# FoX attention scores as two fp32r products over split queries and keys, in a one-layer hybrid decoder

## The chip, the cores and the metric
One core of a Trainium2 chip. The metric is device time in microseconds of one execution, as the median of several runs. Engines are called PE (matrix products), ACT (ScalarE), DVE (VectorE), POOL (GpSimd) and SP (which issues most loads). The core's DMA queues move weights in.

## What is computed
One decoder layer for 512 tokens and a width of 1024, in float32. The input is normed and modulated (adaLN) and goes through one projection into three groups of heads: RWKV-7 (4 heads of 64), FoX (6 heads of 64, forgetting attention) and NSA (6 heads of 64 in two groups; compressed, selected and window branches). Their outputs are concatenated and go through an output projection; a gated feed-forward net with a width-3 convolution follows. The part that this change is about, cut:

```python
def fox_mix(p, b_f):
    q, k, v, f_logit = split_cols(p, FOX_COLS)
    log_f = jax.nn.log_sigmoid((f_logit + b_f))
    cum = jnp.cumsum(log_f, axis=1).transpose(0, 2, 1)
    ...
        logits = (jnp.einsum('bhqd,bhkd->bhqk', qb, k) * scale + cb[..., None] - cum[:, :, None, :])
        probs = masked_softmax(logits, kpos[None, :] <= qpos[:, None])
        return jnp.einsum('bhqk,bhkd->bhqd', probs, v)
...
    x = x + g_m * rmsnorm(y, norm_g[l, 1])     # g_m: "gate 0", a row of silu(c) @ ada_w
```

## The kernel before, in words
Weights are split as they come in: hi is the float32 weight in the reduced format fp32r (ACT, `split`, L182), lo is what remains (DVE or POOL by a letter table, BGE, OPE). A projection is three fp32r products per 128 rows (`mm3`: hi hi, lo hi, hi lo), so 24 products of 512 columns for one 128-wide tile of queries or keys (`fm_gen`).

Three stages follow one another. To 55 us the first projections run. To 208 us the RWKV recurrence runs: preparation, an inversion by doubling (`doubling`, `transition`), then eight chunks for two head pairs (`chunks`), in which PE and DVE take turns on 64 x 64 products. `both` advances this chain and after each step takes BG[n] steps of a background generator (the other projections, compression of NSA keys into `hid` and `kcm`/`vcm`, and `token_major`, whose products are 332 columns wide); LG says how far back in PE's list those steps may be tied. The layer's second modulation (`mods_f`, from `in_ada_c`) also runs here, by a letter table (MFE) on DVE, or on POOL and ACT.

To 395 us the attention runs. Pairs of heads come in the order of AO: NSA 0, then n1, f0, f1, then NSA 2 and FoX 2 with the first part of the output projection. A head is `softmax_t`: scores in four tiles (128, 256, 384 and 512 keys, in three banks `qkps`), a minimum with bias added on DVE (L961), exponentials on ACT (L963), then `transposed_p`: scaling of each tile (SCE, L979), transposes on PE (L985, `ptps`), copies of them to `pt` on ACT or DVE (EVE, L412 and L414), and `pv`. After each softmax `fill` takes FN[n] steps of the query and key projections (`gemms`; later `out_parts`) and GN[n] steps of gate 0 (`gate_pe`).

NSA queries and keys are split in fp32r already (`nsa_gen`, `k_stack`): two products over 128 rows give a tile. FoX queries and keys stay float32 over 64 rows:

```python
            def qk(i, ps, q=q):
                mm(ps, fq[q, i * P:(i + 1) * P], fk[q, :ps.shape[1]], True, False)
                mm(ps[:, i * P:], idr, cmr, False, True)
```

A scheduler that knows priorities puts the instructions of each engine in order; the tables and the order of the code are its input.

Of the kernel before, what the change touches and what calls it, by code (L numbers as in the profile page):

```python
# [11 lines left out]
F32 = mybir.dt.float32  # L12
# [8 lines left out]
BGE = 'DPPDDPDPPDPDDPPPDPPD'  # L21
OPE = 'PPDDPP'
MFE = 'DPPPDDPDPPDDPDPP'
WOE = 'DDP'

SCE = 'DDDD'
EVE = 'ADDA'
# [9 lines left out]
BG = [0, 10, 0, 1, 2, 3, 2, 0, 0, 1, 2, 0, 0, 0, 0, 4, 0, 14, 0, 0, 0, 3, 0, 0, 10, 4, 2, 0, 0, 1, 9, 0, 0, 1, 6, 0, 0, 0, 0, 1, 0, 0, 4, 0, 3, 17, 0, 2, 7, 0, 0, 16, 1, 1, 0, 4, 8, 0, 0, 7, 3, 10, 6, 8, 4]  # L37
LG = [1, 2, 1, -1, 0, -1, -1, -1, -1, -1, -1, 2, -1, 2, -1, -1, 1, -1, -1, -1, -1, -1, 2, 1, -1, -1, 1, -1, -1, -1, -1, -1, -1, 2, -1, -1, 1, 2, 2, 2, -1, 2, 2, 2, 2, -1, -1, -1, -1, -1, -1, -1, -1, -1, -1, -1, -1, 1, -1, 0, 0, 0, 0, 0, 0]
PRI = 400

FN = [11, 4, 12, 6, 6, 1, 13, 13, 14, 0, 10, 12, 15, 9, 17, 8, 26, 14]
GN = [4, 16, 4, 0, 10, 0, 9, 5, 18, 3, 6, 0, 5, 8, 0, 8, 13, 7]
AO = ['n1', 'f0', 'f1']
# [4 lines left out]
P = 128  # L48
S = 512
# [41 lines left out]
def trunk(ctx: ExitStack, tc: tile.TileContext, I, out):  # L91
# [38 lines left out]
    def hh(h):  # L130
        return slice(64 * h, 64 * h + 64)
# [108 lines left out]
    def gate_pe(which, dst, pool):  # L240


        for h in range(2):
            def load(k2):
                return wload(I["ada_g"][which, 2 * k2:2 * k2 + 2, :, 0, 512 * h:512 * h + 512].rearrange("k p c -> p k c"),
                             2, 512)
            raw = [load(0), load(1)]
            yield
            raw.append(load(2))
# [6 lines left out]
            rows = pool.tile([P, 512], F32, name="grow", tag="gacc")  # L256
            nc.scalar.copy(rows, ps)
            yield
            ps = bank("mm")
            mm(ps, ones, rows, True, True)  # L260
            gate_rows(which, h, ps, dst, pool, "gb")
            yield
# [743 lines left out]
    def fox_gen(n, j):  # L1006
# [5 lines left out]
    qz = [at(f"qz{n}", (P, 2, S), 1, F32R) for n in range(2)]  # L1012
    for t in qz:
        for h in range(2):
            nc.gpsimd.memset(t[hh(1 - h), h, :].bitcast(F32), 0.0)
# [21 lines left out]
    def fox(j):  # L1037
# [16 lines left out]
        maps = [softmax_t(maps[0])[0], (fill(), softmax_t(maps[1])[0])[1]]  # L1054
        fill()
# [5 lines left out]
    def nsa(j):  # L1061
# [46 lines left out]
        for br, (kx, vc) in enumerate(((ks, TM_VS), (kw, TM_VW))):  # L1108
            maps = []
            for g in range(2):  # L1110
# [3 lines left out]
                def qk(i, ps):  # L1114
# [3 lines left out]
                    mm(ps, qz[j % 2][:, g, ts], kx[1][:, :w], False, True)  # L1118
# [3 lines left out]
                maps.append((softmax_t((qk, bias, gate[:, :, 3 * h + 1 + br]))[0], vc + g * HD))  # L1122
                fill()
# [419 lines left out]
```

## Time and profile before

| | |
|---|---|
| median of 3 runs (lowest, highest) | 799.06 us (798.9, 800.05) |
| profiled execution: its own time | 799.51 us |
| its span in the trace | 797.7 us |
| mean granted PE clock | 0.981 |
| busy: PE, DVE, ACT, POOL | 94%, 58%, 46%, 16% of the span |

Busy shares are averages over stages. A PE instruction's end is modelled, and products overlap, so the time that one takes from PE is read from the start of the next. A wait is put down to the instruction that came last.

### The profile page before, as it was taken

What the parts mean: (1) busy time and instruction counts of PE and PEld (TensorE: products, weight loads), DVE (VectorE), ACT (ScalarE), POOL (GpSimd) and SP (SyncE); (2) the same over time, 40 slices, a digit from 0 to 9 for tenths busy, and PEclk for the clock granted to TensorE, in tenths of its full rate; (3) what the DMA queues carried; (4) which work ended last, traced back from release to release, by engine and by line L of the source; (5) the groups of instructions that cost most, each with busy time, mean ns of one, the idle gap of its engine ahead of it and who ended that gap; (6) DMA issues with size and microseconds to landing.
All of it is one profiled execution on the core that took longest, in us unless ns stands there. A gap on an engine that the chain in (4) does not pass through costs nothing.

```text
span 797.7 us, 11245 instructions
## 1 busy us (share of the span) xinstructions
PE 750.4 (94%) x4326; PEld 589.6 (74%) x4326; DVE 464.5 (58%) x889; ACT 365.7 (46%) x657; POOL 131.4 (16%) x147
## 2 busy tenths in 40 slices
PE   1999897899898999999999999999999999999996
PEld 0875786789574776566588988888888888888885
DVE  4947896433482663687277676676666575223224
ACT  4658253234573562576255654445444434123121
POOL 3031017143403521002152011111110000000001
PEclk9998998999999998999999999999999999999999
DMA  9961339535216621003144243333233333323302
GB/s 345 396 217 55 92 93 197 196 132 205 76 58 209 200 80 53 27 1 106 55 170 130 82 132 107 132 122 105 98 125 132 106 111 114 98 86 106 101 32 106
DMA packets 38902, 99.49 MB, mean 125 GB/s; under 512 B 13652, under 2 KB 13652, under 8 KB 38848
## 3 DMA queue, kind: packets, MB, share of 16 engines
q1 hardware_dynamic: 33520, 86.88, 32.3%
q0 software_dynamic: 5328, 11.89, 5.1%
q8 instruction: 34, 0.56, 0.3%
q14 instruction: 20, 0.16, 0.1%
HBM read 94.76 MB, written 5.94 MB: 126 GB/s over the span
## 4 chain that ended last, share of the span: by engine, by line
PE 86%; DMA 5%; ACT 3%; DVE 3%; issue 1%; POOL 1%; SPq 0%; DVEq 0%; POOLq 0%; ACTq 0%
PE mmps L104 44%; PE smps L104 13%; PE gmps L104 9%; PE accps L104 7%; PE qkps L104 5%; PE wops L104 5%; PE ptps L985 2%; DMA raw<-in_ada_c 2%; DMA raw<-in_ada_g 1%; DMA x_sb<-in_x 1%; DMA raw<-in_w_fm 1%; ACT whi L182 1%; PE cpps L104 0%; POOL rstd L284 0%; DVE hid L523 0%
## 5 line engine op out<-in xcount | busy, mean ns | idle before, releaser
L182 DVE TENSOR_TENSOR wlo<-raw,whi 128x1024 fp32r<-128x1024 f32 (+2 forms) x86 | 111.6, 1301 | 130.8 <-ACT whi L182 130.5
L182 ACT CAST whi<-raw 128x1024 fp32r<-128x1024 f32 (+3 forms) x102 | 104.3, 1025 | 121.6 <-PE mmps L104 63.5
L104 PE MATMUL mmps<-h2hi,whi 128*128 128x512 f32 (+1 forms) x352 | 133.0, 378 | 0.6 <-ACT h2hi L182 0.6
L104 PE MATMUL mmps<-h2lo,whi 128*128 128x512 f32 (+1 forms) x352 | 132.1, 375 | 0.2 <-DVE h2lo L182 0.2
L104 PE MATMUL mmps<-h2hi,wlo 128*128 128x512 f32 (+1 forms) x352 | 131.9, 375 | 0.0
L104 PEld LDWEIGHTS mmps<-h2hi,whi 128*128 128x128 f32 x352 | 66.2, 188 | 13.2 <-ACT h2hi L182 0.9
L104 PEld LDWEIGHTS mmps<-h2lo,whi 128*128 128x128 f32 x352 | 66.2, 188 | 13.1 <-DVE h2lo L182 0.6
L104 PEld LDWEIGHTS mmps<-h2hi,wlo 128*128 128x128 f32 x352 | 66.2, 188 | 11.9
L182 POOL TENSOR_TENSOR wlo<-raw,whi 128x1024 fp32r<-128x1024 f32 (+2 forms) x16 | 36.9, 2309 | 129.7 <-ACT whi L182 120.7
L272 POOL TENSOR_TENSOR ggf<-ggf,raw 128x1024 f32<-128x1024 f32 x7 | 16.8, 2404 | 145.4 <-ACT raw L271 145.4
L104 PE MATMUL mmps<-whi,hhi 128*128 128x332 f32 (+1 forms) x96 | 34.0, 354 | 0.0
L412 ACT COPY pt<-ptps 128x256 f32<-128x256 f32 (+1 forms) x36 | 16.7, 479 | 37.6 <-PE ptps L985 28.9
L104 PE MATMUL mmps<-whi,hlo 128*128 128x332 f32 (+1 forms) x96 | 33.5, 349 | 0.0
L1396 ACT ACTIVATE gt<-gt 128x512 f32<-128x512 f32 x22 | 13.9, 632 | 42.4 <-DVE gt L1381 42.4
L104 PE MATMUL mmps<-wlo,hhi 128*128 128x332 f32 (+1 forms) x96 | 33.3, 347 | 0.0
L104 PE MATMUL accps<-pt,tm 128*64 128x512 f32 (+3 forms) x144 | 31.0, 442 | 1.4 <-ACT pt L412 1.4
L104 PE MATMUL gmps<-hhi,whi 128*128 128x512 f32 x72 | 30.2, 419 | 1.0 <-ACT nq L1020 1.0
L292 POOL TENSOR_TENSOR rstd<-rstd,mhalf 128x1 f32<-128x1 f32 x8 | 7.0, 873 | 136.6 <-DVE rstd L291 136.6
L104 PE MATMUL gmps<-hlo,whi 128*128 128x512 f32 x72 | 29.0, 402 | 0.0
L104 PE MATMUL gmps<-hhi,wlo 128*128 128x512 f32 x72 | 28.8, 400 | 0.0
L414 DVE COPY pt<-ptps 128x384 f32<-128x384 f32 (+1 forms) x36 | 14.3, 418 | 23.9 <-PE ptps L985 15.4
L225 POOL TENSOR_TENSOR raw<-raw,crow 128x1024 f32<-128x1024 f32 x9 | 21.2, 2366 | 24.9 <-DMA raw<-in_ada_c 23.2
(515 smaller groups left out, 1723.2 us busy)
## 6 DMA issues: line engine op xcount, KB each, us to landing
raw<-in_up SPq DMA_DIRECT2D x44, 512.0 KB, 3.5
raw<-in_ada_c SPq DMA_DIRECT2D x32, 512.0 KB, 9.2
raw<-in_down SPq DMA_DIRECT2D x22, 512.0 KB, 3.4
raw<-in_ada_g SPq DMA_DIRECT2D x16, 512.0 KB, 3.5
raw<-in_w_fm SPq DMA_DIRECT2D x14, 512.0 KB, 5.2
raw<-in_w_out SPq DMA_DIRECT2D x11, 512.0 KB, 3.8
raw<-in_w_k SPq DMA_DIRECT2D x8, 384.0 KB, 9.3
x_sb<-in_x SPq DMA_DIRECT2D x4, 512.0 KB, 9.3
```

The lines of the kernel that those rows point to most:

```text
L104: pe.append(nc.tensor.matmul(o, lhsT, rhs, start=start, stop=stop))
L182: return nc.scalar.copy(hi, src), eng.tensor_tensor(lo, src, hi.bitcast(F32), op=ALU.subtract)
L225: nc.gpsimd.tensor_tensor(raw[n], raw[n], crow, op=ALU.mult)
L272: nc.gpsimd.tensor_tensor(dst, dst, raw, op=ALU.add)
L292: nc.gpsimd.tensor_tensor(r, r, mhalf, op=ALU.pow)
L412: nc.scalar.copy(dst, src)
L414: nc.vector.tensor_copy(dst, src)
L985: nc.tensor.transpose(ps[:, o:o + P], s_[:, kt * P:(kt + 1) * P], ident)
L1396: nc.scalar.activation(gt, gt, AF.Silu)
```

## The change
FoX queries and keys are written as two-half tiles. A query tile holds, for each head of the pair, fp32r queries on the head's 64 rows and their remainder on the other 64. The key tile fk holds the fp32r keys on both halves, fkl the keys' remainder on the head's rows and zeros elsewhere. So fq x fk gives hi hi + lo hi and fq x fkl gives hi lo. fq, fk, qs and qz now have one buffer each, and their writers wait until the previous pair's scores are issued. Gate 0 is made in four quarters of 256 columns, from two loads each that are both asked for a step ahead, rather than in halves from four loads. The order is n0, f0, n1, f1, n2, f2, and all tables are new.

```diff
-BGE = 'DPPDDPDPPDPDDPPPDPPD'
-OPE = 'PPDDPP'
-MFE = 'DPPPDDPDPPDDPDPP'
+BGE = 'PPDDDPPDPDPDDPDPPPDP'
+OPE = 'DDDPDD'
+MFE = 'DDPPPDDDPDDDDPPP'
-SCE = 'DDDD'
-EVE = 'ADDA'
+SCE = 'AAAD'
+EVE = 'AADA'
...
-FN = [11, 4, 12, 6, 6, 1, 13, 13, 14, 0, 10, 12, 15, 9, 17, 8, 26, 14]
-GN = [4, 16, 4, 0, 10, 0, 9, 5, 18, 3, 6, 0, 5, 8, 0, 8, 13, 7]
-AO = ['n1', 'f0', 'f1']
+FN = [11, 0, 11, 9, 17, 1, 24, 4, 22, 0, 15, 22, 26, 6, 16, 23, 34, 19]
+GN = [1, 0, 2, 1, 1, 1, 0, 1, 0, 1, 1, 2, 0, 0, 1, 0, 0, 0]
+AO = ['f0', 'n1', 'f1']
...
-        for h in range(2):
-            def load(k2):
...
-                if k == 6:
-                    raw.append(load(3))
-                mm(ps[g, :], sc32[:, k:k + 1].to_broadcast([P, 32]), raw[k // 2][:, k % 2, :], k < 4, k >= 4)
+        for c in range(4):
+            cs_ = slice(256 * c, 256 * c + 256)
+            raw = [wload(I["ada_g"][which, 4 * n:4 * n + 4, :, 0, cs_].rearrange("k p c -> p k c"), 4, 256) for n in range(2)]
...
+                mm(ps[g, 0:256], sc32[:, k:k + 1].to_broadcast([P, 32]), raw[k // 4][:, k % 4, :], k < 4, k >= 4)
...
+    fkl = at("fkl", (P, 2, S), 1, F32R)
+    qz = at("qz", (P, 2, S), 1, F32R)
...
     def fox_gen(n, j):
         ps = yield from fm_gen(I["w_fm"][(FM_FQ if n == "fq" else FM_FK) + j])
-        t = at(n, (P, S), 2)
-        nc.scalar.activation(t, ps, AF.Copy, scale=-0.125 if n == "fq" else 1.0)
+        while j and ("f", j - 1) not in fqk:
+            yield
+        t = at(n, (P, 2, S), 1, F32R)
+        for h in range(2):
+            src = ps[hh(h), :]
+            if n == "fq":
+                nc.scalar.mul(t[hh(h), h, :], src, -0.125)
+                nc.vector.scalar_tensor_tensor(t[hh(1 - h), h, :], src, -0.125, t[hh(h), h, :].bitcast(F32),
+                                               op0=ALU.mult, op1=ALU.subtract)
+            else:
+                nc.scalar.copy(t[hh(h), h, :], src)
+                nc.scalar.copy(t[hh(1 - h), h, :], src)
+                nc.vector.tensor_tensor(fkl[hh(h), h, :], src, t[hh(h), h, :].bitcast(F32), op=ALU.subtract)
         fqk[n, j] = t
...
-            def qk(i, ps, q=q):
-                mm(ps, fq[q, i * P:(i + 1) * P], fk[q, :ps.shape[1]], True, False)
+            def qk(i, ps, hp=hp):
+                q, w = fq[:, hp, i * P:(i + 1) * P], ps.shape[1]
+                mm(ps, q, fk[:, hp, :w], True, False)
+                mm(ps, q, fkl[:, hp, :w], False, False)
                 mm(ps[:, i * P:], idr, cmr, False, True)
```

First place, PE, the scores of one FoX head (second head of pair 0) and what stands around them. `cmr,idr` is the mask, `ptps` are transposes. Before:

```order
L985 MATMUL ptps<-ident,s__2725 128x128 x3
L104 MATMUL qkps<-fk,fq 128x128
L104 MATMUL qkps<-cmr,idr 128x128
L104 MATMUL qkps<-fk,fq 128x256
L104 MATMUL qkps<-cmr,idr 128x128
L104 MATMUL qkps<-fk,fq 128x384
L104 MATMUL qkps<-cmr,idr 128x128
L104 MATMUL qkps<-fk,fq 128x512
L104 MATMUL qkps<-cmr,idr 128x128
L985 MATMUL ptps<-ident,s__2725 128x128 x4
```

Of the change:

```order
L104 MATMUL qkps<-fk,fq 128x128
L104 MATMUL qkps<-fkl,fq 128x128
L104 MATMUL qkps<-cmr,idr 128x128
L104 MATMUL qkps<-fk,fq 128x256
L104 MATMUL qkps<-fkl,fq 128x256
L104 MATMUL qkps<-cmr,idr 128x128
L104 MATMUL qkps<-fk,fq 128x384
L104 MATMUL qkps<-fkl,fq 128x384
L104 MATMUL qkps<-cmr,idr 128x128
L104 MATMUL qkps<-fk,fq 128x512
L104 MATMUL qkps<-fkl,fq 128x512
L104 MATMUL qkps<-cmr,idr 128x128
```

Each tile has a second product, with fkl, between the first and the mask.

Second place, PE, NSA pair 0, from the last tiles of its second head's scores on (`gmps` is a projection). Before:

```order
L104 MATMUL qkps<-kh,qs 128x384
L104 MATMUL qkps<-lk,qz_2042 128x384
L104 MATMUL qkps<-kh,qs 128x512
L104 MATMUL qkps<-lk,qz_2042 128x512
L104 MATMUL gmps<-hhi,whi 128x512
L104 MATMUL gmps<-hlo,whi 128x512
L104 MATMUL gmps<-hhi,wlo 128x512
```

Of the change:

```order
L104 MATMUL qkps<-kh,qs 128x384
L104 MATMUL qkps<-lk,qz 128x384
L104 MATMUL qkps<-kh,qs 128x512
L104 MATMUL qkps<-lk,qz 128x512
L104 MATMUL qkps<-kh,qs 128x128
L104 MATMUL qkps<-lk,qz 128x128
L104 MATMUL qkps<-kh,qs 128x256
L104 MATMUL qkps<-lk,qz 128x256
```

Before, 20 projection products follow and then the third head; now the third head and most of the fourth follow at once, and 22 projection products after them.

Third place, PE, in the last chunks of the RWKV loop (`s` is the state, `mmps` with 332 columns the filler). Before:

```order
L104 MATMUL smps<-r_1007,mt 64x64
L104 MATMUL smps<-s_1895,tmpa 64x64
L104 MATMUL smps<-r_1007,mt 64x64
L104 MATMUL smps<-s_1895,tmpa 64x64
L104 MATMUL mmps<-whi,hlo 128x332
L104 MATMUL mmps<-whi,hhi 128x332
L104 MATMUL mmps<-wlo,hhi 128x332
L104 MATMUL mmps<-whi,hlo 128x332
```

Of the change:

```order
L104 MATMUL smps<-r_1007,mt 64x64
L104 MATMUL smps<-s_1893,tmpa 64x64
L104 MATMUL smps<-r_1007,mt 64x64
L104 MATMUL smps<-s_1893,tmpa 64x64
L104 MATMUL smps<-tok 64x64
L104 MATMUL smps<-am,tmpb 64x64
L104 MATMUL smps<-tmpb,tok 64x64
L104 MATMUL smps<-am,tok 64x64
```

Ten filler products stand here before and none now. Of the 192 products of 332 columns, 13 stood ahead of the first doubling products, 46 between there and the chunk loop and 133 in the loop; now it is 40, 56 and 96.

## Rows read from the trace of the kernel before

**Rows 1.** The page: busy time, share of the span and instructions of each engine; the chain of work that ended last, by engine.

```profile
PE 750.4 (94%) x4326; PEld 589.6 (74%) x4326; DVE 464.5 (58%) x889; ACT 365.7 (46%) x657; POOL 131.4 (16%) x147
PE 86%; DMA 5%; ACT 3%; DVE 3%; issue 1%; POOL 1%; SPq 0%; DVEq 0%; POOLq 0%; ACTq 0%
```

**Rows 2.** Busy time of each engine in three stages (us from the span's start; instructions in brackets), then the clock, DMA share and GB/s.

```profile
55.00:208.00 153.00, 137.12 (x1466) 112.90 (x1466) 92.08 (x184) 70.70 (x126) 49.32 (x41) 0.94 0.50 146
208.00:395.00 187.00, 180.74 (x868) 119.31 (x868) 110.33 (x351) 100.78 (x248) 32.13 (x47) 0.97 0.25 82
395.00:797.70 402.70, 394.98 (x1838) 328.81 (x1836) 225.70 (x285) 164.01 (x231) 38.71 (x32) 1.00 0.33 110
```

**Rows 3.** What PE waited for, 118 to 208 us: us in total, times, longest.

```profile
PE cpps L104 <- DVE hid L527: 5.2, 1, 5.2
PE smps L104 <- ACT tmpb L791: 2.6, 1, 2.6
```

**Rows 4.** PE's instructions in order of time (start us, us; float32 products stand as two records): the last tile of a FoX head at full clock and what follows, then a head from its first tile to what follows it.

```profile
298.84 1.12 PE L104 MATMUL qkps<-fk,fq 64*128 64x512 f32 x2
299.89 0.33 PE L104 MATMUL qkps<-cmr,idr 128*128 128x128 f32 x1
300.15 1.05 PE L104 MATMUL mmps<-nq,kcm 64*32 64x512 f32 x4
...
303.90 0.48 PE L104 MATMUL qkps<-fk,fq 64*128 64x128 f32 x2
304.32 0.33 PE L104 MATMUL qkps<-cmr,idr 128*128 128x128 f32 x1
...
306.55 1.83 PE L104 MATMUL qkps<-fk,fq 64*128 64x512 f32 x2
308.31 0.47 PE L104 MATMUL qkps<-cmr,idr 128*128 128x128 f32 x1
```

**Rows 5.** The same view: the scores of an NSA head between two projection products.

```profile
228.33 0.39 PE L104 MATMUL gmps<-hlo,whi 128*128 128x512 f32 x1
228.56 0.22 PE L104 MATMUL qkps<-kh,qs 128*128 128x128 f32 x1
228.62 0.28 PE L104 MATMUL qkps<-lk,qz 128*128 128x128 f32 x1
228.73 0.33 PE L104 MATMUL qkps<-kh,qs 128*128 128x256 f32 x1
...
229.83 0.40 PE L104 MATMUL gmps<-hhi,wlo 128*128 128x512 f32 x1
```

**Rows 6.** The same view: gate 0's products (x12 is six float32 products, x4 is two), with PE's idle time ahead of them and what ended it.

```profile
233.99 1.91 PE L104 MATMUL mmps<-raw,sc 128*32 128x512 f32 x12
238.52 1.05 PE L104 MATMUL mmps<-raw,sc 128*32 128x512 f32 x4 [0.23 <-DMA raw<-in_ada_g]
...
250.70 1.05 PE L104 MATMUL mmps<-raw,sc 128*32 128x512 f32 x4 [2.73 <-DMA raw<-in_ada_g]
```

**Rows 7.** What PE waited for, 208 to 395 us: us in total, times, longest.

```profile
PE mmps L104 <- DMA raw<-in_ada_g: 3.0, 2, 2.7
PE accps L104 <- ACT pt L412: 1.4, 3, 0.7
```

**Rows 8.** The instructions on one head's probabilities: ns shortest/median/longest of its four tiles, first and last start, forms.

```profile
L961 DVE CUSTOM_DVE_ANT_0 s__2139<-qkps,bias x4: 292/486/693, 220.8 to 222.2; 128x128 f32<-128x128 f32 x1, 128x256 f32<-128x256 f32 x1, 128x384 f32<-128x384 f32 x1, 128x512 f32<-128x512 f32 x1
L963 ACT ACTIVATE s__2139<-s__2139,mn x4: 402/550/715, 221.2 to 223.4; 128x128 f32<-128x128 f32 x1, 128x256 f32<-128x256 f32 x1, 128x384 f32<-128x384 f32 x1, 128x512 f32<-128x512 f32 x1
L979 DVE TENSOR_SCALAR s__2139<-s__2139,sm x4: 287/380/479, 225.8 to 226.6; 128x128 f32<-128x128 f32 x1, 128x256 f32<-128x256 f32 x1, 128x384 f32<-128x384 f32 x1, 128x512 f32<-128x512 f32 x1
```

**Rows 9.** ACT, 208 to 396 us, groups by form: count, busy us, mean ns of one, idle time before.

```profile
L412 ACT COPY pt<-ptps 128x512 f32<-128x512 f32 x18 | 10.6, 586 | 28.5 <-PE ptps L985 28.4
L412 ACT COPY pt<-ptps 128x256 f32<-128x256 f32 x18 | 6.7, 371 | 9.1 <-PE accps L104 8.5 <-PE ptps L985 0.5
...
L1009 ACT ACTIVATE fq<-gmps 128x512 f32<-128x512 f32 x3 | 1.8, 595 | 4.9 <-PE qkps L104 4.7 <-PE gmps L104 0.2
...
L1083 ACT COPY sp<-mmps 64x512 f32<-64x512 f32 x3 | 1.7, 575 | 3.1 <-PE mmps L104 3.1
```

**Rows 10.** The view of rows 2, in four slices: after the granted clock stand the DMA's share and GB/s.

```profile
136.00:140.00 4.00, 4.00 (x53) 3.58 (x51) 0.39 (x2) 2.46 (x6) 0.00 (x0) 0.55 0.94 266
308.00:312.00 4.00, 4.00 (x14) 3.30 (x14) 1.94 (x9) 2.79 (x8) 0.27 (x1) 0.50 0.00 0
312.00:316.00 4.00, 4.00 (x16) 3.17 (x15) 1.45 (x5) 0.95 (x4) 0.27 (x1) 0.79 0.24 70
372.00:376.00 4.00, 4.00 (x16) 3.25 (x16) 0.82 (x3) 0.63 (x2) 0.00 (x0) 0.61 0.52 188
```

**Rows 11.** PE in order of time, around its two long waits in the RWKV stage.

```profile
135.71 0.43 PE L104 MATMUL cpps<-more,hid 128*32 128x64 f32 x4 [5.19 <-DVE hid L527]
...
151.67 0.31 PE L104 MATMUL mmps<-wlo,hhi 128*128 128x332 f32 x1
151.82 0.31 PE L104 MATMUL mmps<-whi,hlo 128*128 128x332 f32 x1
154.75 1.15 PE L104 MATMUL smps<-mt,tmpb 64*64 64x64 f32 x32 [2.61 <-ACT tmpb L791]
```

**Rows 12.** DVE in order of time: a copy in the chunk loop.

```profile
198.44 0.22 DVE L844 COPY tmpb<-smps 128x64 f32<-128x64 f32 x1 [1.18 <-PE smps L104]
```

More of the change, by code (lines that the diff above doesn't have):

```diff
@@ L240, in gate_pe @@
     def gate_pe(which, dst, pool):
-        for h in range(2):
-            def load(k2):
-                return wload(I["ada_g"][which, 2 * k2:2 * k2 + 2, :, 0, 512 * h:512 * h + 512].rearrange("k p c -> p k c"),
-                             2, 512)
-            raw = [load(0), load(1)]
+        for c in range(4):
+            cs_ = slice(256 * c, 256 * c + 256)
+            raw = [wload(I["ada_g"][which, 4 * n:4 * n + 4, :, 0, cs_].rearrange("k p c -> p k c"), 4, 256) for n in range(2)]
             yield
-            raw.append(load(2))
             ps = bank("mm")
             for k in range(KT):
-                if k == 6:
-                    raw.append(load(3))
                 g = slice(32 * (k % 4), 32 * (k % 4) + 32)
-                mm(ps[g, :], sc32[:, k:k + 1].to_broadcast([P, 32]), raw[k // 2][:, k % 2, :], k < 4, k >= 4)
-            rows = pool.tile([P, 512], F32, name="grow", tag="gacc")
-            nc.scalar.copy(rows, ps)
+                mm(ps[g, 0:256], sc32[:, k:k + 1].to_broadcast([P, 32]), raw[k // 4][:, k % 4, :], k < 4, k >= 4)
+            if c % 2 == 0:
+                rows = pool.tile([P, 512], F32, name="grow", tag="gacc")
+            nc.scalar.copy(rows[:, 256 * (c % 2):256 * (c % 2) + 256], ps[:, 0:256])
             yield
[L259 to L262, printed above, removed]
+            if c % 2:
+                ps = bank("mm")
+                mm(ps, ones, rows, True, True)
+                gate_rows(which, c // 2, ps, dst, pool, "gb")
+                yield
     def gate_pool(which, dst, pool, tag):
@@ L1004, in trunk @@
     fqk = {}
+    fkl = at("fkl", (P, 2, S), 1, F32R)
+    qz = at("qz", (P, 2, S), 1, F32R)
+    for t in (fkl, qz):
+        for h in range(2):
+            nc.gpsimd.memset(t[hh(1 - h), h, :].bitcast(F32), 0.0)
     def fox_gen(n, j):
         ps = yield from fm_gen(I["w_fm"][(FM_FQ if n == "fq" else FM_FK) + j])
-        t = at(n, (P, S), 2)
-        nc.scalar.activation(t, ps, AF.Copy, scale=-0.125 if n == "fq" else 1.0)
+        while j and ("f", j - 1) not in fqk:
+            yield
+        t = at(n, (P, 2, S), 1, F32R)
+        for h in range(2):
+            src = ps[hh(h), :]
[7 more added lines that the diff above has]
+                nc.vector.tensor_tensor(fkl[hh(h), h, :], src, t[hh(h), h, :].bitcast(F32), op=ALU.subtract)
         fqk[n, j] = t
[L1012 to L1015, printed above, removed]
     def nsa_gen(j):
         ps = yield from fm_gen(I["w_fm"][FM_NQ + j])
+        while j and ("n", j - 1) not in fqk:
+            yield
         nq = at("nq", (P, S), 1)
         nc.scalar.mul(nq, ps, -0.125)
-        qs = at("qs", (P, 2, S), 2, F32R)
+        qs = at("qs", (P, 2, S), 1, F32R)
         for h in range(2):
             nc.scalar.copy(qs[hh(h), h, :], nq[hh(h), :])
-            nc.scalar.copy(qz[j % 2][hh(h), h, :], nq[hh(h), :])
+            nc.scalar.copy(qz[hh(h), h, :], nq[hh(h), :])
             nc.vector.tensor_tensor(qs[hh(1 - h), h, :], nq[hh(h), :], qs[hh(h), h, :].bitcast(F32), op=ALU.subtract)
@@ L1054, in fox @@
         maps = [softmax_t(maps[0])[0], (fill(), softmax_t(maps[1])[0])[1]]
+        fqk["f", j] = True
         fill()
@@ L1117, in qk @@
                     mm(ps, qs[:, g, ts], kx[0][:, g, :w], True, False)
[L1118 removed]
+                    mm(ps, qz[:, g, ts], kx[1][:, :w], False, True)
                 def bias(i):
@@ L1122, in nsa @@
                 maps.append((softmax_t((qk, bias, gate[:, :, 3 * h + 1 + br]))[0], vc + g * HD))
+                if br and g:
+                    fqk["n", j] = True
                 fill()
```

5 lines of the change are left out of this document (2 added, 3 removed).

## The prediction
> **What bounds the kernel now.** I read the page first, then the stages, then the waits, then single heads. TensorE (PE) is busy for 94% of the span and the chain of work that ended last runs over PE for 86% of it [rows 1], so whatever leaves PE's list shortens the kernel unless a wait takes its place. The diff touches two of three stages [rows 2]: 55 to 208 us (the RWKV recurrence, with projections as filler) and 208 to 395 us (FoX and NSA attention). What follows 395 us has the same rows in the same order on PE and is taken as unchanged, as are the first 55 us. In the attention stage PE is busy 180.7 of 187 us, ScalarE (ACT) 100.8 and VectorE (DVE) 110.3: PE is the limit with little idle time. In the RWKV stage PE is idle 15.9 of 153 us, and two waits make up half of that [rows 3].
>
> **The FoX scores.** A head's scores are four tiles of 128 to 512 keys. Now each is one float32 product over 64 rows, then the mask product. In a head at a low clock for only its last tile, PE needs 2.65 us from the first tile to the fourth; at full clock the fourth takes 1.05 us and its mask 0.26 us [rows 4]. So a head costs 3.96 us. The two products that replace it already stand in NSA: same format (fp32r), same widths, 128 rows, two per tile. A whole NSA head runs in 1.27 us [rows 5]. I take that for the new FoX head, and add four fp32r masks of 128 columns at the spacing of NSA's 128-wide products (0.06 to 0.11 us, together 0.35 us). The new head costs 1.6 us and saves 2.35 us; six heads save **14.0 us**. The bounds are 7.6 us (first rival) and 16 us (some old heads ran at a lower clock).
>
> The page FP8 and Floating Point Precision of the Trainium skill (TensorE Precision Notes) says that true FP32 takes four passes through the array. By passes alone an old head would be twice an NSA head's time, 2.54 us, and the gain over six heads 7.6 us, an estimate by that page. The rows give 3.96 us, masks included, so the trace holds more than the passes.
>
> **Gate 0.** A group of six products takes 1.9 us and one of two takes 1.05 us [rows 6]: about 1 us for up to four products, which go to four strips of 32 output rows. Both halves make 5.9 us. Now there are four quarters, each two groups of four at half the width: 4 x 2 x 0.5 = 4.2 us at most. That saves **1.7 us** (bounds 0 and 2.5). PE also waited 3.0 us for these loads [rows 6, 7]. Each quarter's loads are now asked for a step ahead, but quarters 0 and 1 stand only one FoX head (1.6 us) and some transposes apart and there are three raw buffers, so I count half of the wait as saved, **1.5 us** (0 to 3).
>
> **What is added beside PE.** The tables move three of four scalings of each head (SCE) and the 128-wide copy of P transposed (EVE) from DVE to ACT, and the queries and keys are now split there. ACT copies of 512 and 256 columns take 0.586 and 0.371 us [rows 9], a slope that puts 384, 256 and 128 columns at 0.48, 0.37 and 0.26 us, 1.11 us for a head's three scalings. The nearest ACT instruction with a factor per row is the exponential, whose lower three widths (0.40 us at 128 to 0.72 us at 512, [rows 8]) would make 1.5 us. Eighteen heads: 20 to 27 us. The 128-wide copies add 18 x 0.26 = 4.8 us. Splitting adds 18 copies of 64 x 512 at 0.575 us and drops six at 0.595 us [rows 9]: 6.8 us. ACT gains 32 to 39 us, I take 35: 136 us in a stage of some 175 us. DVE loses about 15 us net, the same scalings being 0.29 to 0.48 us there [rows 8]; the three w_out splits that go from GpSimd (POOL) to DVE stay within that.
>
> With 86 idle us on ACT before and some 39 after, not all of this stays hidden. I price the new waits of PE at **+7 us**, in three places. First, the scores of three NSA heads now follow one another with no projection between (second order excerpt): a head's reductions on DVE take 0.29 to 0.69 us each, 1.95 us in all [rows 8], against 1.27 us on PE, and there are three score banks; 2 us (0 to 3). Second, the first FoX head needs fkl, which DVE makes after ACT's copy of the same half; both stand behind what their queues already hold, and only a score tile, transposes and a gate group lie between the key projection and its use: 1.5 us. Third, the transposes of a head now wait for scalings that stand in ACT's queue behind other heads' exponentials: a tenth of the 35 us, 3.5 us. Bounds: 2 us (the projections cover nearly all) and 35 us (none is covered; a rival).
>
> What I cost at nothing: single buffers for fq, fk, qs and qz, since their writers wait only for a previous head pair's scores, and the order shows whole projections (24 products, 5.5 us) elsewhere in between; with that cover gone it would be a projection's evacuation, 2.3 us, five times. FoX 0 now stands before NSA 1, so its bias must come through DRAM sooner: POOL's stores and loads of it move ahead of NSA 1's table loads. Between the transposes of the gate logits and the next FoX products stand a projection (24 x 0.23 us, [rows 5]) and PV products, over 5.5 us, which cover a scan and two short transfers; without cover 5 us.
>
> **The clock.** Four slices of 4 us ran at 0.50 to 0.79 of the clock although PE was busy all through [rows 10]; beside the full clock they cost 0.45 x 4 + 0.50 x 4 + 0.21 x 4 + 0.39 x 4 = 6.2 us. Three follow FoX scores. If half-filled float32 products set this off, they are gone; but PE will also wait more. I take **2 us** gained (0 to 6).
>
> **The RWKV stage.** Before the first doubling products there were 13 projection products of 332 columns, now 40. These 27, at 0.15 us each [rows 11], fill 4.1 of the 5.2 us in which PE waited for hid. Between there and the chunk loop 56 stand in place of 46, in front of the second wait (2.6 us, for ACT's tmpb [rows 3, 11]): 24 of them in one group where 8 were; 2.4 us. The chunk loop keeps 96 of 133, and its last three chunks have none (third order excerpt). A bare step there waits for a DVE copy of 0.22 us [rows 12] and its two semaphores, some 0.3 us, and six bare steps cost 2 us. Net **4.5 us** gained; bounds are 8 us (all of both waits) and 3 us lost. SP's loads are asked for in nearly the same order. POOL's split of the second w_tm part now stands ahead of the loads of the inverted tiles; 2.3 us of POOL work, hidden by those 27 products, and 2 us if it isn't.
>
> **Sum.** 14.0 + 1.7 + 1.5 - 7 + 2 + 4.5 = 16.7 us gained. The profiled execution took 799.5 us (span 797.7 and 1.8 around it), which gives 782.8; the median of the runs is 0.45 lower, so **782.5 us**. A measurement of this kernel can tell about 0.2% (1.6 us) from no change.
>
> **Rivals.**
> (a) Only the passes go: what float32 costs over four passes is due to switching formats around the scores and remains. Against it: NSA heads among the same neighbours run 1.27 us. For it: the switch to float32 transposes is still there. FoX gains 7.6, not 14.0: 789 us.
> (b) The bare tail of the chunk loop and the waiting ACT cost more than the filler gains: the RWKV stage gets 3 us longer rather than 4.5 us shorter. For it: 37 fewer filler products in a loop of DVE and PE turns; against it: those two waits. 790 us.
> (c) The low clocks go entirely and all of the gate's wait too: 4 + 1.5 us more. For it: three slow slices follow FoX scores. 777 us. TensorE: Matmul & The Clock Gate of the Trainium skill (Part 1) says that the clock falls after an idle window of about 3.4 us; by it FoX products on a busy PE would not set it off and this gain would be missing. The slices [rows 10] show full busy time at 0.50, so the trace does not settle it.
> (d) Slower: ACT, working through its queue in order, becomes the bound. If every head's transposes wait out its three scalings and the copy, that is 18 x 1.56 = 28 us, and 28 - 3.5 more than forecast makes 807 us. It decides from 13 of the 18 heads: up to there the 20.2 us gained before this wait still cover it. For it: ACT at four fifths of the stage. Against it: 288 projection products of 0.23 us [rows 5] that can stand between.
> (e) The change doesn't do what it says: masks and split products with new weights for each keep the head near 4 us, and filler is only moved. 799 us. NSA's rows speak against it.
>
> **How the numbers follow.** Forecast 0.58 (777 to 789 alone), (a) 0.10, (b) 0.14, (c) 0.10, (d) 0.05, (e) 0.03. The range 773 to 794 takes in (a), (b) and (c) with their uncertainty and leaves out (d), (e) and some edges. Faster: 0.92. Within 0.2%: (e), 0.03. Slower: (d), 0.05.
>
> **What would show it.** FoX tiles of 512 keys at about 0.45 us for both products, a head at 1.6 us; no float32 products in qkps. Gate groups of 0.5 us. PE idle before cpps from hid below 1.5 us, and small idle times in the last three chunks. ACT near 136 us in the attention stage and PE waits on ACT of some 5 us there (1.4 for pt before, [rows 7]). The forecast is wrong if that stage stays above 182 us: then ACT (its pt or scaling line as the releaser) or the reductions took PE's place; or if the stage before it doesn't shorten.

## The result, and the profile after

The median is 771.58 us (771.12 to 777.23 in four runs), against 798.98 us for the kernel before beside it: a ratio of 0.9675 (of the means, 772.88 and 798.82 us), with a 95% interval of 0.9627 to 0.9723. The gain of the medians is 27.4 us where 16.7 were forecast; 771.58 us lies 1.4 us beyond the fast end of the range, and the mean 0.1 us. The profiled execution took 771.4 us, with a span of 769.6 and a mean granted clock of 0.990. The trace accounts for 28.1 us of span.

The page after the change answers to [rows 1]: busy time by engine, then the chain that ended last.

```profile
PE 728.3 (95%) x4358; PEld 584.7 (76%) x4358; DVE 453.1 (59%) x836; ACT 393.3 (51%) x739; POOL 120.5 (16%) x142
PE 86%; DVE 5%; DMA 3%; ACT 2%; issue 2%; POOL 1%; SPq 0%; DVEq 0%; POOLq 0%; ACTq 0%
```

PE has 32 instructions more and 22 us less to do; ACT gained 28 us and stays far from the bound. Next, busy time by stage, as in [rows 2]: attention, the recurrence before it, the rest. The last lines are three stretches of the chunk loop that are used below.

```profile
199.00:367.00 168.00, 162.66 (x901) 115.67 (x900) 97.56 (x294) 131.47 (x335) 24.16 (x42) 1.00 0.29 91
55.00:199.00 144.00, 133.39 (x1466) 111.63 (x1464) 94.76 (x189) 68.11 (x121) 46.26 (x43) 0.95 0.54 160
367.00:769.60 402.60, 394.85 (x1838) 328.83 (x1836) 225.67 (x285) 163.54 (x231) 38.51 (x32) 1.00 0.33 110
176.00:192.00 16.00, 16.00 (x248) 15.08 (x248) 5.75 (x16) 8.77 (x16) 9.24 (x5) 1.00 0.61 200
160.00:164.00 4.00, 1.42 (x19) 1.08 (x19) 2.04 (x5) 0.39 (x1) 0.00 (x0) 0.94 0.88 324
164.00:168.00 4.00, 4.00 (x59) 3.68 (x58) 2.24 (x7) 1.15 (x2) 2.35 (x1) 0.63 0.80 247
```

By the first projection product of the attention stage and the first product of the output projection, attention went from 187.3 to 167.8 us (19.4 less), what stands ahead of it from 207.9 to 199.2 us (8.7 less), and the rest is unchanged at 402.6 us. PE is idle 5.3 us in the attention stage, where it was 6.3, but ACT does 131 us of work there where it did 101, and the granted clock of the stage is 1.00 where it was 0.97.

What PE waited for in the attention stage, against [rows 7] (us in total, times, longest):

```profile
PE qkps L104 <- DVE mn L958: 2.4, 2, 1.3
PE mmps L104 <- ACT nq L1033: 1.4, 1, 1.4
PE accps L104 <- ACT pt L409: 0.7, 1, 0.7
PE gmps L104 <- DVE fq L1020: 0.6, 1, 0.6
```

The wait on gate 0's loads (3.0 us in [rows 7]) is gone, and no wait on ACT's added scalings has come. A FoX head and a quarter of gate 0, PE in order of time, against [rows 4, 6]:

```profile
228.74 1.07 PE L104 MATMUL mmps<-raw,sc 128*32 128x256 f32 x16
229.74 0.33 PE L104 MATMUL qkps<-fk,fq 128*128 128x128 f32 x1
...
343.77 0.31 PE L104 MATMUL qkps<-fk,fq 128*128 128x128 f32 x1
343.92 0.28 PE L104 MATMUL qkps<-fkl,fq 128*128 128x128 f32 x1
344.03 0.27 PE L104 MATMUL qkps<-cmr,idr 128*128 128x128 f32 x1
...
344.95 0.45 PE L104 MATMUL qkps<-fk,fq 128*128 128x512 f32 x1
345.24 0.39 PE L104 MATMUL qkps<-fkl,fq 128*128 128x512 f32 x1
345.47 0.22 PE L104 MATMUL qkps<-cmr,idr 128*128 128x128 f32 x1
345.53 0.44 PE L104 MATMUL gmps<-whi,hhi 128*128 128x512 f32 x1
```

Start to start, the tile of 512 keys takes 0.52 us for both products, and this head 1.76 us (343.77 to 345.53) where an old one took 3.96. A gate quarter takes 1.0 us.

To set the two kernels side by side I gave each PE instruction of the attention stage the time from its start to the next start, less the idle time that the trace puts ahead of the next, and summed by kind (us):

| | before | after | differs |
|---|---|---|---|
| FoX scores and masks | 24.0 | 11.0 | -13.0 |
| gate 0, products and rows | 7.1 | 6.0 | -1.1 |
| projections (the same 288 products) | 72.1 | 68.2 | -3.9 |
| transposes of P | 22.8 | 20.8 | -2.0 |
| NSA scores | 16.5 | 18.2 | +1.7 |
| PV and others | 38.5 | 38.3 | -0.2 |
| idle: gate loads | 3.0 | 0.0 | -3.0 |
| idle: all else | 3.3 | 5.3 | +2.0 |

Ahead of the attention stage PE was idle 33.2 us before and 28.1 after, and its products took 3.5 us less. Three of its waits there, the first two new and the third to be set against [rows 3]:

```profile
PE smps L104 <- DVE tmpb L841: 2.6, 1, 2.6
PE smps L104 <- DVE s L854: 1.3, 1, 1.3
PE cpps L104 <- DVE hid L524: 1.3, 1, 1.3
```

In every trace of this case the granted clock is either 1.00 or 0.50, and up to the output projection each fall lasts 3.41 us, or two or three times that. Counted in stretches of 3.41 us, one costs a busy PE 1.7 us; values in between come from slices of 4 us that hold a part of one. By the record of the clock the attention stage had three slow stretches before (two in a row from 306.8 to 313.7 us and one from 371.7 to 375.1), 5.1 us in all, of which 1.1 fell on the FoX scores, 3.3 on the projections and 0.7 on the transposes. After the change it has none. From 55 us to the attention stage there were five and are now four.

### The profile page after: what moved, and what is told of

The parts are those of the page before. It is cut to its first block, busy times and chain, and to the rows that moved or that the text cites. A ratio compares the mean times of both kernels' runs of the same rounds, so it can differ in the third digit from the quotient of the medians.

```text
span 769.6 us, 11350 instructions
## 1 busy us (share of the span) xinstructions
PE 728.3 (95%) x4358; PEld 584.7 (76%) x4358; DVE 453.1 (59%) x836; ACT 393.3 (51%) x739; POOL 120.5 (16%) x142
## 4 chain that ended last, share of the span: by engine, by line
PE 86%; DVE 5%; DMA 3%; ACT 2%; issue 2%; POOL 1%; SPq 0%; DVEq 0%; POOLq 0%; ACTq 0%
PE mmps L104 44%; PE smps L104 13%; PE gmps L104 9%; PE accps L104 8%; PE wops L104 4%; PE qkps L104 3%; PE ptps L982 3%; DMA raw<-in_ada_c 2%; DMA x_sb<-in_x 1%; DVE wlo L182 1%; DVE hid L519 1%; ACT whi L182 1%; PE cpps L104 1%; DVE raw L222 0%; POOL rstd L281 0%
## 5 line engine op out<-in xcount | busy, mean ns | idle before, releaser
L182 DVE TENSOR_TENSOR wlo<-raw,whi 128x1024 fp32r<-128x1024 f32 (+2 forms) x89 | 116.3, 1310 | 136.9 <-ACT whi L182 136.6
L104 PEld LDWEIGHTS mmps<-h2hi,wlo 128*128 128x128 f32 x352 | 66.2, 188 | 11.8
L182 POOL TENSOR_TENSOR wlo<-raw,whi 128x1024 fp32r<-128x1024 f32 (+2 forms) x13 | 31.4, 2413 | 120.4 <-ACT whi L182 77.8
L409 ACT COPY pt<-ptps 128x256 f32<-128x256 f32 (+2 forms) x54 | 19.9, 410 | 15.4 <-PE ptps L982 12.9
L182 ACT CAST ahi<-gt 128x512 fp32r<-128x512 f32 x14 | 8.7, 620 | 34.2 <-DVE gt L1414 34.2
L104 PEld LDWEIGHTS accps<-pt,tm 128*64 128x64 f32 x144 | 14.0, 136 | 11.9 <-issue 6.4
```

The costliest lines, as they stand in the source:

```text
L104: pe.append(nc.tensor.matmul(o, lhsT, rhs, start=start, stop=stop))
L182: return nc.scalar.copy(hi, src), eng.tensor_tensor(lo, src, hi.bitcast(F32), op=ALU.subtract)
L409: nc.scalar.copy(dst, src)
```

## Experiments

The kernels were timed in three groups, each beside the kernel before (medians 798.98, 799.59 and 799.97 us). Where parts of the change are undone, the comparison is the change's 771.58 us.

### 1. The FoX scores alone

```diff
-            def qk(i, ps, q=q):
-                mm(ps, fq[q, i * P:(i + 1) * P], fk[q, :ps.shape[1]], True, False)
+            def qk(i, ps, hp=hp):
+                q, w = fq[:, hp, i * P:(i + 1) * P], ps.shape[1]
+                mm(ps, q, fk[:, hp, :w], True, False)
+                mm(ps, q, fkl[:, hp, :w], False, False)
```

Not shown: the split tiles of `fox_gen` and the single buffers, as in the change.

> The kernel before with the FoX scores alone changed: two fp32r products over 128 rows, with the split queries and keys and single buffers; all tables, the order of heads and gate 0 stay. Theory 1 (the low clock in the attention stage belongs to the old scores): by the two traces the score products fall from 24.0 us in all to 11.0, and the 4-us slices below 0.9 in the attention stage, which lost about 5 us (some 1.3 of that inside the scores), disappear: 13 + 4 = 17 us gained, 782 us, no slice below 0.95 between 208 us and the output projection. Rival 1 (the clock falls for another reason, as waits or the order of the heads): the slow slices stay, 13 us gained, 786 us. Rival 2 (the forecast's price of 14.0 us for the scores, then 2 for the clock): 783 us. Rival 3 (only passes go): 7.6 us gained, 791 us.

Measured: 793.03 us, ratio 0.9925 (0.9901 to 0.9949): 6 us gained, less than any theory gave. The scores themselves fell to 10.9 us as theory 1 had it, so rival 3's price of them is out too: the price was right and the sum wrong. What PE waited for from 205 us on:

```profile
PE ptps L985 <- DVE pt L414: 3.0, 4, 1.2
PE mmps L104 <- DMA raw<-in_ada_g: 2.9, 2, 2.5
PE qkps L104 <- DVE mn L961: 1.5, 2, 1.2
PE accps L104 <- ACT pt L412: 1.3, 3, 0.7
```

PE's idle time in the stage is 11.8 us, against 6.2 before: with the scores shorter, DVE's copies of transposed P and its reductions come late. The attention stage took 180.4 us, 6.9 less than before; what stands ahead of it, where nothing was changed, took 209.2 us, 1.3 more, with one slow stretch more. The slow slices at the FoX heads are gone, as theory 1 said, but there is a new one behind the wait on the gate's loads (the view of rows 2 in two slices of 4 us):

```profile
252.00:256.00 4.00, 1.45 (x5) 0.19 (x4) 0.69 (x1) 0.58 (x1) 0.54 (x1) 0.82 1.01 372
256.00:260.00 4.00, 4.00 (x20) 1.95 (x18) 0.00 (x0) 2.48 (x3) 1.75 (x1) 0.75 0.60 182
```

### 2. The tables of the recurrence alone

Edit: BGE, MFE, BG and LG as in the change.

> The kernel before with four tables of the change alone (BGE, MFE, BG, LG: engines of the weight splits and of the second modulation, and the background steps in the recurrence). Theory 1: the stage up to the first attention projection becomes 8.7 us shorter, as in the change, whose other parts touch nothing there: 790.3 us, wait for hid 1.3 us, no slow clock at 132 to 140 us. Rival 1 (the forecast's term): 4.5 us shorter, 794.5 us, the rest having come from other parts of the change. Rival 2 (the filler that was moved out of the chunk loop is missed in the attention stage): 8.7 us gained and some given back there, 792 to 796 us.

Measured: 790.18 us, ratio 0.9909 (0.9878 to 0.9940): 8.8 us gained at the median, the time of theory 1. Its ten runs spread from 787.5 to 797.0 us, so the exact figure is luck. The profiled one took 795.75 us. In it, what stands ahead of the attention stage took 200.9 us, 7.0 less than before and not 8.7: PE's wait for hid was 1.3 us as said, but one slow stretch more falls there than in the change. The attention stage took 190.6 us, 3.3 more than before; it has six slices below 0.9 of the clock (five slow stretches, where the kernel before has three), each in or right behind a float32 FoX head.

### 3. Gate 0 by quarters alone

Edit: `gate_pe` and GN as in the change.

> The kernel before with gate 0 by quarters and the table of its steps (GN) alone. Theory 1 (the loads' wait goes whole, as in the change's trace): 3.0 us of wait and 1.1 us of products gained, 794.9 us, no wait on these loads above 0.3 us. Rival 1 (the forecast: half of the wait stays): 1.5 + 1.7 = 3.2 us, 795.8 us, with a wait on the loads of 1 to 2 us. Rival 2 (the wait was hidden idle time and comes back at another place in the stage): under 1.5 us gained, 797.5 to 799 us.

Measured: 800.10 us, ratio 1.0018 (0.9990 to 1.0045): nothing gained, rival 2's result. Its reason can be read. The loads' wait did go, but the scheduler put other work ahead of the first NSA queries on ACT. PE (the last line) and ACT (the others), in order of time:

```profile
214.56 0.22 ACT L1151 ACTIVATE f<-f 128x24 f32<-128x24 f32 x1 [4.99 <-DVE f L1150]
214.68 1.03 ACT L182 CAST whi<-raw 128x1024 fp32r<-128x1024 f32 x1
215.73 1.28 ACT L1155 ACT_TABLE_LOAD   x1
217.02 0.22 ACT L1155 ACTIVATE f<-f 128x24 f32<-128x24 f32 x1
217.15 0.58 ACT L1017 ACTIVATE nq<-gmps 128x512 f32<-128x512 f32 x1
217.78 1.92 PE L104 MATMUL mmps<-nq,kcm 64*32 64x512 f32 x4 [4.97 <-ACT nq L1017]
```

The projection ended at 212.8 us. Its evacuation (nq) stands in ACT's queue behind an exponential of FoX's forget gate, for whose operand ACT waited on DVE until 214.56 us, a weight split, a table load and a logarithm. The wait of 0.7 us became 5.0, and the products behind it ran at about half clock (1.92 us for what took 1.05).

### 4. Float32 scores over 128 rows

```diff
-                mm(ps, fq[q, i * P:(i + 1) * P], fk[q, :ps.shape[1]], True, False)
+                mm(ps, fq[:, hp, i * P:(i + 1) * P], fk[:, :ps.shape[1]], True, False)
```

with fq as a tile of two halves, zero where the other head's rows are.

> The kernel before with FoX scores still as one float32 product per tile, but over 128 rows: each head's queries stand over 64 rows of zeros, the keys of both heads of the pair fill the other operand. Same results, same passes, twice the rows; queries have one buffer. Theory 1 (the clock falls where PE runs for some 6 us on products that fill half of its rows or columns: PV products and a float32 head stand in a row ahead of both slow stretches): the tile of 512 keys still takes about 1.05 us at full clock, the slow slices at 304 to 316 and 368 to 376 us go, about 5 us gained, 794 us. Rival 1 (float32 products lower the clock however many rows they fill): slow slices as before, 799 us. Rival 2 (the clock has nothing to do with the scores): slow slices as before, 799 us, told from rival 1 by the first experiment.

Measured: 791.53 us, ratio 0.9916 (0.9891 to 0.9940), 7.5 us gained. The time is beyond what theory 1 gave, and its price of the tile was wrong: the scores fell from 24.0 to 15.6 us although every pass of float32 was kept. One head, PE in order of time, to be compared with [rows 4]:

```profile
291.24 0.39 PE L104 MATMUL qkps<-fk,fqz 128*128 128x128 f32 x2
291.39 0.31 PE L104 MATMUL qkps<-cmr,idr 128*128 128x128 f32 x1
...
292.83 1.07 PE L104 MATMUL qkps<-fk,fqz 128*128 128x512 f32 x2
293.34 0.62 PE L104 MATMUL qkps<-cmr,idr 128*128 128x128 f32 x1
293.80 0.60 PE L985 MATMUL ptps<-ident,s__2707 128*128 128x128 f32 x4
```

(The mask's start lies inside the product's last pass here, so tile and mask are read together.) The tile of 512 keys and its mask take 0.97 us (292.83 to 293.80) where they took 1.31; the head 2.56 us where it took 3.96. It is 0.33 to 0.39 us less for each tile, whatever its width. No slow slice is left around the FoX heads.

### 5. The change with float32 scores over 64 rows

Edit: `fox_gen` and `qk` of FoX as before, one buffer each, in the changed kernel.

> The changed kernel with the FoX scores back as one float32 product over 64 rows per tile (single buffers, all tables and the rest of the change stay). Theory 1 (the scores are worth their PE time and the clock; the tables of the change keep PE fed, which the tables of before did not when the FoX scores alone were changed and PE's idle time grew from 6.2 to 11.8 us): scores 11.0 to 24 us, two slow stretches of about 2 us each come back, 771.6 + 13 + 4 = 789 us. Rival 1 (the scores are worth only what they brought alone, 6 us, since waits cover the rest): 777.6 us, with PE's idle time in the attention stage well below the change's 5.3 us. Rival 2 (no slow stretch comes back): 784.6 us.

Measured: 790.0 us, 18.4 us slower than the change. That is theory 1's number by another route: the scores go up by 12.2 us, and no slow stretch comes back at the FoX heads (rival 2's part). The rest is a wait of 5.0 us for the first NSA queries in place of 1.4, the same as in experiment 3, with slow slices behind it. From 260.3 to 268.5 us one FoX head stands between PV products of 64 columns and the compressed logits (64 rows), 8 us in which only the masks fill the array, and the clock stays whole:

```profile
260.00:264.00 4.00, 4.00 (x22) 1.87 (x21) 1.97 (x9) 1.64 (x7) 3.90 (x4) 1.00 0.88 252
264.00:268.00 4.00, 4.00 (x15) 1.75 (x14) 2.53 (x10) 4.00 (x13) 2.56 (x10) 1.00 0.93 320
```

### 6. The change with the letters SCE and EVE of before

> The changed kernel with the letters for scaling and copying the probabilities as before (SCE all on DVE, EVE 'ADDA'): some 25 us of work go from ACT back to DVE. Theory 1 (the move to ACT is what keeps DVE from holding up PE: with the new scores and the old letters PE waited 3.0 us for DVE's pt copies and 1.5 us for its reductions): 2 to 5 us slower, 774 to 777 us, with PE waiting on DVE for pt. Rival 1 (the forecast: a tenth of the added ACT work shows as waits, so taking it away gains): 3.5 us faster, 768 us. Rival 2 (the letters do not matter): 771.6 us, within 1 us.

Measured: 783.0 us, 11.4 us slower: theory 1's sign, at twice its size. PE's idle time in the stage is 11.1 us. FoX scores, 1.4 us longer, and transposes, 1.4 us longer, are cut apart more; one slow stretch follows from 261.3 us on. So in this order the work that went to ACT is not a price that was paid: it is worth over 11 us in its place. Theory 1's mechanism shows only in part: PE waits just 0.6 us for DVE's copies to pt; of the 5.7 us of idle time that came, 1.3 are on DVE's reductions, 2.0 on copies to pt that ACT makes and 1.0 on DVE's fkl. Its largest waits of PE:

```profile
PE qkps L104 <- DVE mn L958: 3.7, 3, 1.3
PE accps L104 <- ACT pt L409: 2.3, 3, 1.1
```

### 7. The change with gate 0 by halves

Edit: `gate_pe` as before, GN = [1, 0, 0, 1, 1, 1, 0, 0, 0, 0, 1, 1, 0, 0, 0, 0, 0, 0].

> The changed kernel with gate 0 by halves from four loads as before, its steps placed at the fills where the quarters' steps stand. Theory 1 (the quarters with both loads asked for ahead removed the wait): products 1.1 us longer and a wait on the loads of 2.5 to 3 us in each or one of the halves, 775 to 776 us. Rival 1 (the tables alone hide the loads; quarters alone gained nothing in the kernel before): 1.1 us longer, 772.7 us, no wait. Rival 2 (gate 0 does not matter at all): 771.6 us.

Measured: 787.0 us, 15.4 us slower, which no theory had. Gate 0 itself costs 1.5 us more and waits for no load. The rest is how everything else falls: idle time 11.3 us (4.5 of it on the reductions in six places, with DVE and ACT busy all through), and the clock falls behind waits of 1.1 to 2.0 us in three places, four slow stretches in all. Two of the slices:

```profile
224.00:228.00 4.00, 3.46 (x9) 2.49 (x9) 2.62 (x9) 3.84 (x11) 0.00 (x0) 0.50 0.00 0
...
336.00:340.00 4.00, 2.54 (x13) 1.52 (x14) 3.78 (x15) 3.94 (x13) 0.00 (x0) 0.81 0.00 0
```

### 8. No mask products

Edit: the line `mm(ps[:, i * P:], idr, cmr, False, True)` is taken out, so the computation lacks the causal mask.

> The kernel before without the mask products of the FoX scores (24 products over 128 rows of 128 columns; the causal mask is left out of the computation), so that the float32 products over 64 rows follow one another. Filling all 128 rows took 0.36 us off each tile together with its mask. Theory 1 (that 0.36 us is the change between 64 and 128 rows and back, around each mask): tiles in a row are spaced 0.23, 0.46, 0.68 and 0.91 us, four passes each, a head costs some 2.5 us and the scores in all 15 to 17 us in place of 24.0. Rival (a product over 64 rows is dearer by itself): the tile of 512 keys still takes 1.05 us among its like, a head 2.9 to 3.0 us, 18 to 19 us in all.

Measured: the scores take 14.9 us (one run, 790.79 us), 9.1 less, the masks' own time included. That is theory 1: what cost 0.36 us in each tile is going from 64 rows to 128 for the mask and back. The eight records of a whole head now run in 2.35 us, four passes of 1280 columns:

```profile
306.13 2.42 PE L104 MATMUL qkps<-fk,fq 64*128 64x128 f32 x8
308.48 0.66 PE L985 MATMUL ptps<-ident,s__2725 128*128 128x128 f32 x4
```

### 9 and 10. The scores with the letters, and with the letters, AO and FN

> The kernel before with the new FoX scores and the letters SCE and EVE of the change, and nothing else. The scores alone gained 6 us at the median where PE's score time fell by 13.1 us: PE's idle time in the attention stage grew from 6.2 to 11.8 us, 3.0 of it on DVE's pt copies and 1.5 on its reductions. Theory 1 (DVE is what held PE up, and the letters relieve it): PE's waits on pt copies and reductions fall to the change's 3 us or less, idle time near 7 us, 4 to 6 us faster than with the scores alone: 787 to 789 us. Rival (the waits come from the order in which the heads and the filler stand, and letters do not matter by themselves): 792 to 794 us, idle time above 10 us. Rival 2 (the added ACT work now holds PE): slower than with the scores alone, 795 us or more.

> As the kernel with the new FoX scores and the letters SCE and EVE, and with the order of heads (AO) and the filler's table (FN) of the change too; gate 0 and the recurrence's tables stay as before. Theory 1 (the order lets the projections cover the waits; what then lacks is gate 0): the attention stage at the change's 167.8 us plus the gate's 1.4 us of products and its wait of 3 us, 172 us, in all 783 to 784 us. Rival (the order needs the gate's quarters to fall into place, as the halves put back cost 15 us): attention at 178 us or more, 789 us or more.

Measured: 799.4 us, ratio 0.9989 (0.9966 to 1.0012), and 801.25 us, ratio 1.0012 (0.9995 to 1.0029). Both main theories fail: with the letters, and with the order too, the kernel is slower than with the scores alone (793.0). What came is rival 2 of experiment 9, ACT holding PE, and the rival of experiment 10 (its attention stage took 188.3 us). Idle time in the attention stage is 14.1 and 17.4 us. With the letters the waits move to ACT:

```profile
PE accps L104 <- ACT pt L412: 3.5, 4, 1.1
PE mmps L104 <- DMA raw<-in_ada_g: 2.9, 2, 2.7
PE qkps L104 <- DVE mn L961: 2.7, 5, 1.2
PE ptps L985 <- ACT pt L412: 2.4, 5, 0.8
```

With the order too, the first FoX head's bias comes late through DRAM. POOL, DVE and PE (the last line) in order of time:

```profile
268.02 3.54 POOL L182 TENSOR_TENSOR wlo<-raw,whi 128x1024 fp32r<-128x1024 f32 x1 [4.87 <-ACT whi L182]
271.50 0.53 POOL L1190 DMA_DIRECT2D dcum<-bias  x1
275.43 1.12 POOL L1058 DMA_DIRECT2D bias<-dcum  x2 [3.40 <-DMA dcum<-bias]
279.12 0.29 DVE L961 CUSTOM_DVE_ANT_0 s__2561<-qkps,bias 128x128 f32<-128x128 f32 x1 [6.30 <-DMA bias<-dcum]
279.82 0.48 PE L104 MATMUL qkps<-fk,fq 128*128 128x128 f32 x1 [3.47 <-DVE mn L961]
```

DVE's scan was done at 268.7 us, but POOL, which stores it, had begun a weight split at 268.0. In the change that store stands 0.3 us behind the scan. This is the cover that the prediction named for the bias, gone, at 3.5 us.

### 11 and 12. The tables of the recurrence in two pieces

> The kernel before with the letters of the weight splits (BGE) of the change alone. By the order of instructions this alone puts 40 projection products in place of 13 ahead of PE's wait for hid, and 102 in place of 132 into the chunk loop; the background steps (BG, LG) move nothing there. Theory 1 (the wait for hid is filled, 3.9 us, and with it goes the low clock that follows it, 2 to 3 us; the other waits stay): 792 to 793.5 us, no slice below 0.9 between 132 and 140 us. Rival 1 (only the wait, the clock falls at the next wait instead): 795 us. Rival 2 (the loop misses the filler): 797 us or more.

> The kernel before with the background steps (BG, LG) of the change alone, the complement of the experiment on BGE, but for MFE. Theory 1 (the gain of the four tables, 8.8 us, comes from the split letters): under 2 us either way, 797 to 801 us, the wait for hid still 5 us. Rival (steps and letters give about half each): 794 to 796 us.

Measured: 805.64 us, ratio 1.0080 (1.0043 to 1.0117), for the split letters; 799.77 us, ratio 1.0018 (0.9993 to 1.0042), for the steps. So 6 us lost and nothing, where both and MFE together gain 8.8. The letters alone do put 40 products ahead of hid, but that wait is still 3.2 us, and new ones on DVE stand behind it (mt 3.1, tmpa 1.9, state 1.7 us), with eight slow stretches where five were. Theory 1 of experiment 11 fails, and its rival 2, that the loop misses the filler, has the sign and the range. Theory 1 of experiment 12 holds only for its own time, and that is a balance: in the profiled execution the part ahead of the attention stage took 4.7 us more (eight slow stretches), the attention stage 3.2 us less. There the FoX scores are untouched and yet no slow stretch stands at their heads; at the full clock they take 23.0 us.

## Why the prediction was right, and where its sizes were not

**FoX scores, 14.0 forecast, 13.0 found.** The mechanism and almost the size are right; a head is 1.83 us in the mean where 1.6 was forecast, and 1.76 where nothing stands between its tiles. What the step left unnamed is the cause. Experiment 4 keeps float32 and fills the rows, and 8.4 of the 13.0 us go: 1.1 of them are slow stretches inside the old scores, the other 7.3 the changes between 64 and 128 rows. Experiment 8 gets 9.1 us, the masks' own time included, by leaving out the products between which they change. The 4.6 us that remain are left for the passes. Rival (a) had it the wrong way round: what lay beyond the passes was a switch, but of rows and not of formats, and it went with the rows. TensorEngine Tiling (Array Packing) of the Trainium skill (Key Properties) says that a change of the tiling mode drains TensorE; the traces don't show the drain itself, but agree in that two changes cost 0.33 to 0.39 us in a tile.

**Gate 0, 1.7 + 1.5 forecast, 1.1 + 3.0 found.** The wait went whole, since both loads of a quarter are asked for a step ahead. But that term cannot be had by itself: experiments 3 and 7. (Three products in the prediction are loose, none by more than 0.2 us: 4 x 2 x 0.5 is 4.0, and its 4.2 takes half of 1.05 for a group; 18 x 0.26 is 4.7; 782.8 less 0.45 is 782.4.)

**New waits, +7 forecast, +2.0 found.** Of the three places mainly the first showed: 2.4 us on reductions against 2. fkl cost nothing (a wait of 0.6 us is on DVE's split of fq), nor did the scalings in ACT's queue, where 3.5 us were set (the wait on pt fell from 1.4 to 0.7 us). The step failed by pricing ACT's added work, 31 us where 35 were set, as a load of which a tenth must show. Its sign depends on the order: taken back in the change it cost 11.4 us (experiment 6), put beside the new scores in the old order it cost 5 to 6 us, with PE waiting 5.9 us for ACT's copies (experiment 9). NSA scores, which got 1.7 us dearer, stand in no term; they take 18.2 us in experiment 1 too, whose order of heads is the old one, so the new order is not the cause, which stays open.

**The clock, 2 forecast, 4 found.** The stage lost its three slow stretches, 5.1 us, of which 4.0 are outside the scores: most of the 3.9 us on the projections, the same 288 products, and 0.7 of the 2.0 us on transposes. That is near the upper bound, and rival (c)'s case. How much of it belongs to the change is less sure than the sum: with the old scores the stage lost 5.1 us (before), 8.5 (experiment 2) and 1.7 (experiment 12).

**The recurrence, 4.5 forecast, 8.7 found.** The two fillings came as worked out: hid 3.9 us (4.1), ACT's tmpb 2.6 us (2.4). The bare tail of the chunk loop did not cost 2 us: the last filler product starts at 186.9 us, and up to 192 us PE is busy all through (the line for 176 to 192 us). New are two waits in the middle of the loop, 2.6 and 1.3 us, behind the first of which the slow slice at 164 us begins; against them 2.5 us of small waits are gone. The step missed that PE's products there get cheaper by 3.5 us. Half of it, 1.7 us, is on the 192 filler products, and 0.8 of that is the clock, as more of them stood in slow stretches before. The rest fits the price of a change of rows. The filler stands in 14 groups in place of 19, mostly among products over 64 rows, and ahead of the attention stage neighbouring products change their rows 39 times where they changed 51 times: six pairs, an estimate of 2.0 to 2.3 us by the price above. Other traces go along. Less what they lost to the clock, the products ahead of the attention stage take 167.5 and 167.6 us with 51 and 53 changes (before, experiment 12), and 163.7 to 164.2 us with 39 to 41 (the change, experiments 2 and 11). All of the latter have the new letters of the weight splits, so rows are not told from letters: this cause is likely and not shown.

**The sum.** It took the parts as independent, and the experiments show that they are not. Alone, scores, tables and gate bring 6.0, 8.8 and -1.1 us at the medians, 13.7 of the 27.4. Undone alone, scores, letters and gate cost 18.4, 11.4 and 15.4 us. Each part moves the instructions of all engines. PE's idle time in the attention stage is 5 us in the change and 11 to 17 in the mixtures of experiments 1, 6, 7, 9 and 10, and each of these has one to four slow stretches there, where the change has none. The way that the forecast gave is right, and its terms for the scores and the two fillings are right in mechanism and size; that the whole came out is in part luck. By its own prices experiment 10 would have gained some 9 us (14.0 - 7 + 2) and it gained nothing, so the sum has no term that tells such a mixture from the change. The errors for the waits, the recurrence and the clock (5.0, 4.2 and 2.0 us) all lie on the cautious side. Rival (d) was real in kind in experiment 9, where PE waits for ACT, and not in the change. Which part of the tables' fit makes the last 13.7 us is not settled: no single part does. The order alone, the change without the tables of the recurrence, and the change with float32 scores over 128 rows were not tried.

## What to carry to other kernels

Look at how many rows neighbouring products use: a short product over 128 rows between products over 64 costs the change twice, and filling the rows with zeros can pay more than a cheaper format. When PE's work shrinks, ask first which engine now comes late. Whether moving work off that engine pays depends on the order around it: the same letters were worth 11 us in the changed order and cost 5 to 6 us in the old one. A reordering is judged whole: a piece of a tuned set of tables, tried alone, says little about the set.

## What the runs showed of the hardware beyond that

Float32 takes four passes: a whole head of 1280 columns runs in 2.35 us (experiment 8), 0.94 us for 512 columns, against 0.23 us of an fp32r product. FP8 and Floating Point Precision of the Trainium skill (TensorE Precision Notes) says the same; it held as soon as the change of rows was out of the way.

The slow stretches stand behind PE waits of 2.5 to 5 us (experiments 1, 3, 5, 9, 10) and of 1.1 to 2.0 (6, 7), and also inside runs of float32 heads and PV products with no wait at all [rows 10]. But the wait of 2.7 us that ends at 250.7 us [rows 6] was followed by none in the kernel before, and by one in experiments 1 and 9. TensorE: Matmul & The Clock Gate of the Trainium skill (Part 1) tells of an idle window of some 3.4 us that runs freely. The length of the stretches, 3.41 us, agrees with it, and so does that the same wait, or much the same run of half-filled products (experiment 5), is followed by a fall in one execution and not in another; the falls behind 2.5 us of idle time and less, and at a busy PE, are outside its rule. What fills such a window enough is open. No fall stands at the FoX heads where rows are filled (experiment 4) or the mask is left out (experiment 8), but none does in experiments 5 and 12 either, which keep half-filled rows and masks, so one trace of each doesn't show what ended the falls. As one stretch more or less is 1.7 us, differences of that size between single executions can be the clock's alone.
